# Convolution's tokens and attention's latents, 32 bytes further on in SBUF

## The chip, the cores and the metric

The kernel runs on one core of a Trainium2 chip. The metric is the device time of one execution, in microseconds (us). The engines are TensorE (PE; its weight loads, PEld, overlap its matmuls), VectorE (DVE), ScalarE (ACT), GpSimd (POOL) and SyncE (SP), which issues most of the DMAs. A matmul holds one operand still in the array (the stationary one, loaded by a weight load ahead of it) and streams the other (the moving one) past it. Both are read from SBUF.

## The reference

Two layers act on 256 tokens of width 2048, all in float32. The first layer mixes tokens with a Conformer convolution module, the second with multi-head latent attention; each is followed by an MLP with a squared ReLU.

```
x = x + conv_module(rms_norm(x))     # layer 0
x = x + sq_relu_mlp(rms_norm(x))
x = x + mla(rms_norm(x))             # layer 1
x = x + sq_relu_mlp(rms_norm(x))
return rms_norm(x)

conv_module:  u = h @ w_pw1 + b; u = a * sigmoid(gate)      # 2048 -> 2 x 2048
              u = causal depthwise conv, width 31
              u = silu(layer_norm(u)) @ w_pw2 + b
mla:          down = h @ w_in                               # c_q 512, c_kv 512, k_pe 64
              q  = rms_norm(c_q)  @ w_q_up                  # 16 heads x (128 + 64)
              kv = rms_norm(c_kv) @ w_kv_up                 # 16 heads x (128 + 128)
              softmax of (q_nope k_nope + q_pe k_pe), block-causal mask; @ v; @ w_o
sq_relu_mlp:  square(relu(h @ w1)) @ w2                     # 2048 -> 8192 -> 2048
```

## The kernel before

**Split products.** Every large product is made of float32r parts. A weight tile comes in by DMA (`raw`), ScalarE copies it to a rounded high part `hi`, and VectorE or GpSimd writes the remainder `lo = raw - hi`. The tokens have a high and a low part likewise. A product is then three matmuls: high by high, high by low, low by high. The pool `wpool` holds six `hi` and six `lo` buffers of 4096 bytes per partition.

**Turned tokens.** `open_xt` opens a pool on the right side of SBUF with four tiles `xt` of 8192 bytes per partition; `xh(k)` and `xl(k)` are the high and low parts of the k-th 128 channels for all 256 tokens. `to_T` fills them: TensorE turns 128x128 blocks against `ident`, ScalarE writes the high part (L201), VectorE the low one (L208). The pool is opened once at the start, and serves the convolution's first product, the first MLP and attention's first product. It is closed when attention opens its own right-hand pool `gp`, and opened again for the last MLP.

**Convolution.** The loop runs over 16 chunks c of 128 channels. For a chunk, `conv_mm` (L850 to L852) does 96 matmuls of 256 columns: 16 slices of the width, two halves (value and gate), three products; the weights stand still and `xh(k)` or `xl(k)` moves. `glu` makes the gated row `ub` from the two sums (ScalarE L872 and L880, GpSimd L881; for the last chunk VectorE L875). VectorE then does most of the 31 taps of the depthwise convolution (L952), after ScalarE has started the sum with tap 0 (L908) and some taps have gone to ScalarE and GpSimd (L885, L928, joined at L935). GpSimd writes nearly all low parts of the weights here (L170). Up to some 20 taps of earlier chunks may be left over (`REST`), and `to_tokens(c - 3)` (L990) lets TensorE turn a finished chunk between the matmuls of chunk c. The last chunk's taps are partly done by TensorE (L900). After the layer norm comes the second product, with 512 moving columns of weights (L195 to L197), whose results are added to the residual stream and prepared for the MLP as `xt` again.

**MLP.** Upwards, `xh` with `xl` (512 columns, L510) and `xh` alone (256 columns, L508) move past the weights. Downwards weights move (512 columns).

**Attention.** The first product has `xt` stationary and moves weights, in two halves of 288 columns for keys and values and 512 for queries. The normed latents are turned into `kvh`, `kvl` (keys and values) and `qh`, `ql` (queries), 128 x 4 x 256 each. From these come the keys of each head (L1412 to L1414: weights stationary, `kvh` and `kvl` moving), the queries (L1435 to L1437, `qh` and `ql` moving), and, through `mm3` (L195 to L197), values and rotary queries (the latents stationary, 256 columns of weights moving). `kpA`, `kpB` and `qpB` hold the rotary key with the mask, and the rotary query. The pieces of the next group of four heads are placed by hand between the scores of the current one.

**Placement.** Several pads fix where tiles start: `PAD_CONST`, `PAD_SMALL` and `PAD_RIGHT` in the outer pools, `PAD_SH` and `PAD_STATS` in the convolution's, `PAD_O` ahead of attention's outputs `oh` and `ol`. With the sizes of all tiles added up, `hi`, `lo`, `xt`, `sh`, `kvh`, `kvl`, `qh`, `ql`, `oh` and the MLP's tiles begin at addresses whose remainder modulo 256 is 64. A right-hand pool ends where the tile `pad_right` begins, and its tiles lie in it in the order in which they are made, so a tile made behind them moves them to lower addresses. The order of instructions on each engine is that of the program text (`manual_schedule`).

Of the kernel before, what the change touches and what calls it, by code (L numbers as in the profile page):

```python
# [10 lines left out]
F32 = mybir.dt.float32  # L11
# [7 lines left out]
P = 128  # L19
# [17 lines left out]
PAD_CONST = 24  # L37
PAD_SMALL = 32
PAD_RIGHT = 40
PAD_SH = 16  # L40
PAD_STATS = 48
PAD_O = 64
WB = 6
LOOK = WB // 2 - 1
LAST_PE = 22
# [37 lines left out]
def trunk_kernel(  # L83
# [49 lines left out]
    edge = ctx.enter_context(tc.tile_pool(name="edge", bufs=1, side="right"))  # L133
    pad_right = edge.tile([P, PAD_RIGHT], F32, name="pad_right")
    nc.gpsimd.memset(pad_right, 0.0)
# [3 lines left out]
    def nm(s):  # L139
        uid[0] += 1  # L140
        return f"{s}_{uid[0]}"
# [104 lines left out]
    def to_T(src, k0, hi, lo, gain, pt=None):  # L246

        pt = pt if pt is not None else tr_tile()
        for j in range(2):
            for t in range(T):  # L250
                nc.tensor.transpose(  # L251
                    pt[:, j * S + t * P : j * S + (t + 1) * P],
                    src[:, t, (k0 + j) * P : (k0 + j + 1) * P],
                    ident,
                )
        ps = [pt[:, j * S : (j + 1) * S] for j in range(2)]
        for j in range(2):
            hi_part(ps[j], hi(k0 + j), gain[:, k0 + j : k0 + j + 1])
        for j in range(2):
            lo_part(ps[j], hi(k0 + j), lo(k0 + j), gain[:, k0 + j : k0 + j + 1])  # L260
# [44 lines left out]
    def right_pool(name, bufs):  # L305

        xt_cx[0].close()
        xt_cx[0] = ExitStack()
        return xt_cx[0].enter_context(tc.tile_pool(name=name, bufs=bufs, side="right", reuse_waits="tile"))

    ctx.callback(lambda: xt_cx[0].close())

    def open_xt(name):
        pool = right_pool(name, 1)
        xt[:] = [
            pool.tile([P, KC // NNB, 2 * S], F32R, name=nm("xt")) for _ in range(NNB)
        ]

    xhl = lambda k: xt[k // 4][:, k % 4, :]
    xh = lambda k: xhl(k)[:, :S]  # L320
    xl = lambda k: xhl(k)[:, S:]
    open_xt("xt0")
    spare = []

    xh_kt = lambda k, t: xh(k)[:, t * P : (t + 1) * P]
# [2 lines left out]
    def residual_stage(last, gain, r_scale=None):  # L328


        ssq = small.tile([P, T, NNB], F32, tag="ssq", name=nm("ssq")) if last else None

        def add(n, ps, t):
            sl = slice(n * NB, (n + 1) * NB)
            if r_scale is None:
                nc.vector.tensor_tensor(xs[:, t, sl], ps[t], xs[:, t, sl], op=ALU.add)
            else:
                nc.vector.scalar_tensor_tensor(
                    out=xs[:, t, sl], in0=ps[t], scalar=r_scale[:, t : t + 1], in1=xs[:, t, sl],
                    op0=ALU.mult, op1=ALU.add,  # L340
                )

        def prepare(n, only=None):
            sl = slice(n * NB, (n + 1) * NB)
            if last:
                if gain is not None:
                    for j in range(2):
                        to_T(xs, 4 * n + 2 * j, xh, xl, gain)
                for t in range(T) if only is None else [only]:
                    nc.scalar.activation(spare[-1](), xs[:, t, sl], AF.Square, accum_out=ssq[:, t, n : n + 1])  # L350

        return ssq, add, prepare
# [441 lines left out]
    with ExitStack() as cx:  # L794
# [15 lines left out]
        cn = cv.tile([P, T, D], F32, tag="tok", name="cn")  # L810
        cv.tile([P, PAD_SH], F32, name="pad_sh")
        sh = cv.tile([P, KC, S], F32R, name="sh")
# [204 lines left out]
        with tc.manual_schedule():  # L1017
# [143 lines left out]
            for m in range(NP):  # L1161
# [17 lines left out]
                sl = slice(i * NB, (i + 1) * NB)  # L1179
                nc.vector.tensor_tensor(xs[:, t, sl], xs[:, t, sl], b2[:, sl], op=ALU.add)  # L1180

        ssq, add, prepare = residual_stage(True, g_mlp[0])
        for b in range(2):
            for t in range(T):
# [62 lines left out]
    with ExitStack() as cx:  # L1247
        at = cx.enter_context(tc.tile_pool(name="at", bufs=1, reuse_waits="tile"))
# [60 lines left out]
        def u_load(n):  # L1309
            if n < len(units):  # L1310
                srcs, shape = units[n]
                raw = raws[n] = wpool.tile(shape, F32, tag="raw", name=nm("raw"), bufs=3)
                for i, src in enumerate(srcs):
                    dst = raw if len(srcs) == 1 else raw[:, i : i + 1, :]
                    if len(src.shape) == 4:
                        dst = dst.rearrange("p j (h n) -> p j h n", h=src.shape[2])
                    nc.sync.dma_start(dst, src)
# [18 lines left out]
        def prefetch(n=9):  # L1336
            while pending and n > 0:
# [3 lines left out]
                if h == 1:  # L1341
                    u_load(u + 3)

        kvh = at.tile([P, KR // P, S], F32R, name="kvh")
        kvl = at.tile([P, KR // P, S], F32R, name="kvl")
        qh = at.tile([P, QR // P, S], F32R, name="qh")
# [15 lines left out]
        for i in range(2):  # L1362
            for j in range(HG):
                nc.scalar.activation(qpB[i][DR:, j, :], mq[DR:, :], AF.Copy)
        pad_o = at.tile([P, PAD_O], F32, name="pad_o")
        nc.gpsimd.memset(pad_o, 0.0)
# [202 lines left out]
        with tc.manual_schedule():  # L1569
# [123 lines left out]
            prefetch()  # L1693

        open_xt("xt1")
        ssq, add, prepare = residual_stage(True, g_mlp[1])
        for b in range(2):
# [82 lines left out]
```

## Time and profile before

| | us |
|---|---|
| median of 3 runs | 1940.86 |
| lowest, highest | 1940.85, 1940.98 |
| profiled execution | 1940.68 |
| its span | 1938.9 |

| engine | busy us | share of the span |
|---|---|---|
| TensorE matmuls | 1915.4 | 99% |
| TensorE weight loads | 1682.5 | 87% |
| VectorE | 1651.8 | 85% |
| ScalarE | 1204.8 | 62% |
| GpSimd | 223.7 | 12% |

The mean granted clock of TensorE was 0.998. The convolution's first product and taps fill some 20 to 220 us of the span, its second product the time up to some 320 us, the first MLP the time up to some 990 us, attention that up to some 1260 us, and the second MLP the rest.

A row of a group gives line, engine, operation, the tiles (out<-in), the shapes and the count, then the time in which any of them ran, the mean length of one in ns, and the engine's idle time ahead of them with what ended it. Matmuls overlap in the pipeline, so the mean length of one is more than its share of the time; the distance between starts, read from the timeline (start, length, engine, line, tiles, count), is that share. A row of windows gives the stretch, its length and the busy time of each engine, with the number of instructions.

### The profile page before, as it was taken

To read this page: it belongs to the slowest core of one execution; us is meant where nothing else is said; L and a number is where in the kernel's file an instruction comes from. 1 tells how busy PE (TensorE), PEld (TensorE's weight loads), DVE (VectorE), ACT (ScalarE), POOL (GpSimd) and SP (SyncE) were. 2 spreads that over 40 slices of the span, in tenths; PEclk is the share of its full clock that TensorE was granted. 3 is DMA by queue.
4 is the path that set the end of the run, shared out by engine and by line. 5 is a ranking of instruction groups with operands and counts; after the bars stand their busy time and mean duration, and the time that the engine had idled before them with its cause. 6 is when DMAs were issued, how large, how long until landed. Compare 5 with 4: busy or idle time off the path is not lost.

```text
span 1938.9 us, 28476 instructions
## 1 busy us (share of the span) xinstructions
PE 1915.4 (99%) x10778; PEld 1682.5 (87%) x10778; DVE 1651.8 (85%) x2372; ACT 1204.8 (62%) x1709; POOL 223.7 (12%) x183
## 2 busy tenths in 40 slices
PE   7999999999999999999999999999999999999998
PEld 7999888888888888888899998888888888888886
DVE  5999875789999999999976666557999999999887
ACT  5556654766666666666566665556766666666654
POOL 5999400000000000000001410000000000000000
PEclk9999999999999999999999999999999999999999
DMA  8666456857666667666646445765667666766663
GB/s 236 184 175 177 146 184 169 222 171 210 198 204 204 203 198 212 200 198 212 199 143 182 121 152 174 200 186 171 201 191 210 210 196 195 214 200 195 211 223 109
DMA packets 407113, 367.62 MB, mean 190 GB/s; under 512 B 15416, under 2 KB 351936, under 8 KB 406720
## 3 DMA queue, kind: packets, MB, share of 16 engines
q1 hardware_dynamic: 405952, 363.63, 62.8%
q10 hardware_dynamic: 1024, 2.17, 0.3%
q8 instruction: 84, 1.38, 0.3%
q14 instruction: 53, 0.43, 0.1%
HBM read 363.68 MB, written 2.10 MB: 189 GB/s over the span
## 4 chain that ended last, share of the span: by engine, by line
PE 98%; DVE 1%; DMA 1%; ACT 0%; issue 0%; DVEq 0%; ACTq 0%
PE acc L510 24%; PE acc L196 15%; PE acc L195 15%; PE acc L197 15%; PE acc L508 13%; PE acc L851 3%; PE acc L850 3%; PE acc L852 3%; PE acc L251 1%; PE sum L900 1%; PE acc L1435 0%; PE acc L1437 0%; PE acc L1436 0%; PE acc L1412 0%; PE acc L1414 0%; PE acc L1413 0%
## 5 line engine op out<-in xcount | busy, mean ns | idle before, releaser
L421 DVE TENSOR_TENSOR lo<-raw,hi 128x1024 fp32r<-128x1024 f32 (+1 forms) x512 | 571.1, 1122 | 90.1 <-ACT hi L420 81.7
L420 ACT ACTIVATE hi<-raw 128x1024 fp32r<-128x1024 f32 (+1 forms) x512 | 479.7, 970 | 66.9 <-PE acc L196 66.6
L510 PE MATMUL acc<-xt,hi 128*128 128x512 f32 x2048 | 503.2, 391 | 0.0
L510 PEld LDWEIGHTS acc<-xt,hi 128*128 128x128 f32 x2048 | 376.1, 188 | 72.5
L195 PE MATMUL acc<-hi,sh 128*128 128x512 f32 x930 | 362.7, 390 | 0.0
L197 PE MATMUL acc<-lo,sh 128*128 128x512 f32 x930 | 362.0, 389 | 0.0
L196 PE MATMUL acc<-hi,sl 128*128 128x512 f32 x802 | 312.0, 389 | 0.0
L508 PEld LDWEIGHTS acc<-xt,lo 128*128 128x128 f32 x2048 | 262.6, 191 | 10.0
L508 PE MATMUL acc<-xt,lo 128*128 128x256 f32 x2048 | 265.7, 283 | 0.0
L169 ACT ACTIVATE hi<-raw 128x1024 fp32r<-128x1024 f32 (+2 forms) x184 | 179.8, 1005 | 46.8 <-PE acc L196 43.0
L197 PEld LDWEIGHTS acc<-lo,sh 128*128 128x128 f32 x930 | 174.6, 188 | 36.2
L195 PEld LDWEIGHTS acc<-hi,sh 128*128 128x128 f32 x930 | 174.6, 188 | 36.0
L170 DVE TENSOR_TENSOR lo<-raw,hi 128x1024 fp32r<-128x1024 f32 (+2 forms) x118 | 132.8, 1146 | 68.5 <-ACT hi L169 62.8
L420 ACT ACTIVATE hi<-V 128x1024 fp32r<-128x1024 f32 x94 | 99.5, 1059 | 129.6 <-DVE V L716 114.8
L196 PEld LDWEIGHTS acc<-hi,sl 128*128 128x128 f32 x802 | 150.5, 188 | 31.2
L952 DVE SCALAR_TENSOR_TENSOR sum<-ub,w_dw,sum 128x256 f32<-128x256 f32 x400 | 163.3, 482 | 8.7 <-ACT sum L908 7.1
L170 POOL TENSOR_TENSOR lo<-raw,hi 128x1024 fp32r<-128x1024 f32 x66 | 157.7, 2409 | 24.4 <-ACT hi L169 24.4
L420 ACT ACTIVATE hi<-T 128x1024 fp32r<-128x1024 f32 x94 | 99.2, 1056 | 89.6 <-DVE T L704 77.2
L515 ACT ACTIVATE U<-acc 128x512 f32<-128x512 f32 x128 | 76.0, 593 | 117.6 <-PE acc L510 117.0
L850 PE MATMUL acc<-xt,hi 128*128 128x256 f32 x512 | 146.3, 286 | 0.0
L851 PE MATMUL acc<-xt,hi 128*128 128x256 f32 x512 | 145.0, 283 | 0.3 <-DVE xt L208 0.3
L852 PE MATMUL acc<-xt,lo 128*128 128x256 f32 x512 | 144.9, 283 | 0.0
(269 smaller groups left out, 2805.5 us busy)
## 6 DMA issues: line engine op xcount, KB each, us to landing
raw<-in_mlp_w SPq DMA_DIRECT2D x256, 1024.0 KB, 6.1
raw<-in_conv_w_pw SPq DMA_DIRECT2D x64, 512.0 KB, 5.5
raw<-in_conv_w_pw SPq DMA_DIRECT2D x16, 1024.0 KB, 5.1
raw<-in_mla_w_o SPq DMA_DIRECT2D x16, 1024.0 KB, 5.3
raw<-in_mla_w_kv_up SPq DMA_DIRECT2D x8, 1024.0 KB, 5.4
raw<-in_mla_w_in SPq DMA_DIRECT2D x8, 576.0 KB, 3.8
raw<-in_mla_w_in SPq DMA_DIRECT2D x4, 1024.0 KB, 7.1
raw<-in_mla_w_q_up SPq DMA_DIRECT2D x16, 256.0 KB, 5.1
```

The lines of the kernel that those rows point to most:

```text
L169: nc.scalar.activation(hi, raw[:, js, :], AF.Copy)
L170: eng.tensor_tensor(lo, raw[:, js, :], hi.bitcast(F32), op=ALU.subtract)
L195: nc.tensor.matmul(ps, sh, mh, start=start, stop=False)
L196: nc.tensor.matmul(ps, sl, mh, start=False, stop=False)
L197: nc.tensor.matmul(ps, sh, ml, start=False, stop=stop)
L420: nc.scalar.activation(parts[0], src, AF.Copy)
L421: nc.vector.tensor_tensor(parts[1], src, parts[0].bitcast(F32), op=ALU.subtract)
L508: nc.tensor.matmul(ps[0][:, :S], wl[:, j, :], xh(k), start=False, stop=False)
L510: nc.tensor.matmul(ps[0], wh[:, j, :], xhl(k), start=k == 0, stop=k == KC - 1)
L850: nc.tensor.matmul(o, wh[:, bs], xh(k), start=k == 0, stop=False)
L851: nc.tensor.matmul(o, wh[:, bs], xl(k), start=False, stop=False)
L852: nc.tensor.matmul(o, wl[:, bs], xh(k), start=False, stop=k == KC - 1)
```

## The change

The constant `PAD_XT` (56 floats, 224 bytes) and `PAD_KV` (8 floats, 32 bytes) are new, and `PAD_O` goes from 64 to 56 floats.

For the convolution the right-hand pool is now opened under the name `xtc`, with a pad tile behind the four `xt` tiles, which puts them 224 bytes lower: at remainder 96 modulo 256, 32 more than that of `hi` and `lo`. Ahead of the second product's additions to the residual stream the pool is closed and a new one, `xt0`, opened without a pad, so the MLP's and attention's `xt` stand where they stood before.

In attention, a pad of 32 bytes stands ahead of `kvh`, so `kvh`, `kvl`, `qh`, `ql`, `kpA`, `kpB` and the two `qpB` move up by 32 bytes, to remainder 96; `pad_o` is 32 bytes shorter, so `oh`, `ol` and all that follows stay where they were. The weights stay at 64. No matmul, copy or DMA is added or removed.

```
+PAD_XT = 56
+PAD_KV = 8
-PAD_O = 64
+PAD_O = 56
...
-    def open_xt(name):
+    def open_xt(name, pad=0):
         pool = right_pool(name, 1)
         xt[:] = [
             pool.tile([P, KC // NNB, 2 * S], F32R, name=nm("xt")) for _ in range(NNB)
         ]
+        if pad:
+            pool.tile([P, pad], F32, name=nm("pad_xt"))
...
-    open_xt("xt0")
+    open_xt("xtc", PAD_XT)
...
+        open_xt("xt0")
         ssq, add, prepare = residual_stage(True, g_mlp[0])
         for b in range(2):
             for t in range(T):
...
+        at.tile([P, PAD_KV], F32, name="pad_kv")
         kvh = at.tile([P, KR // P, S], F32R, name="kvh")
         kvl = at.tile([P, KR // P, S], F32R, name="kvl")
         qh = at.tile([P, QR // P, S], F32R, name="qh")
```

More of the change, by code (lines that the diff above doesn't have):

```diff
@@ L39 @@
 PAD_RIGHT = 40
+PAD_XT = 56
+PAD_KV = 8
 PAD_SH = 16
 PAD_STATS = 48
-PAD_O = 64
+PAD_O = 56
 WB = 6
@@ L311, in trunk_kernel, with open_xt @@
     ctx.callback(lambda: xt_cx[0].close())
-    def open_xt(name):
+    def open_xt(name, pad=0):
         pool = right_pool(name, 1)
@@ L317, in open_xt @@
         ]
+        if pad:
+            pool.tile([P, pad], F32, name=nm("pad_xt"))
     xhl = lambda k: xt[k // 4][:, k % 4, :]
@@ L321, in trunk_kernel @@
     xl = lambda k: xhl(k)[:, S:]
-    open_xt("xt0")
+    open_xt("xtc", PAD_XT)
     spare = []
@@ L1180, in trunk_kernel @@
                 nc.vector.tensor_tensor(xs[:, t, sl], xs[:, t, sl], b2[:, sl], op=ALU.add)
+        open_xt("xt0")
         ssq, add, prepare = residual_stage(True, g_mlp[0])
@@ L1342, in prefetch @@
                     u_load(u + 3)
+        at.tile([P, PAD_KV], F32, name="pad_kv")
         kvh = at.tile([P, KR // P, S], F32R, name="kvh")
```

## The prediction

> **What bounds the kernel.** I read the page first: its busy shares and the chain of work that ended last.
>
> ```profile
> PE 1915.4 (99%) x10778; PEld 1682.5 (87%) x10778; DVE 1651.8 (85%) x2372; ACT 1204.8 (62%) x1709; POOL 223.7 (12%) x183
> PE 98%; DVE 1%; DMA 1%; ACT 0%; issue 0%; DVEq 0%; ACTq 0%
> PE acc L510 24%; PE acc L196 15%; PE acc L195 15%; PE acc L197 15%; PE acc L508 13%; PE acc L851 3%; PE acc L850 3%; PE acc L852 3%; PE acc L251 1%; PE sum L900 1%; PE acc L1435 0%; PE acc L1437 0%; PE acc L1436 0%; PE acc L1412 0%; PE acc L1414 0%; PE acc L1413 0%
> ```
>
> TensorE is busy for 99% of the span and carries 98% of the chain, so a change of some nanoseconds in its matmuls counts wherever nothing else is equally full. The change does no arithmetic; it moves operands by 32 bytes, so the question is which matmuls it touches and what each costs from start to start. The groups by shape give the counts:
>
> ```profile
> L850 PE MATMUL acc<-xt,hi 128*128 128x256 f32 x512 | 146.3, 286 | 0.0
> L851 PE MATMUL acc<-xt,hi 128*128 128x256 f32 x512 | 145.0, 283 | 0.3 <-DVE xt L208 0.3
> L852 PE MATMUL acc<-xt,lo 128*128 128x256 f32 x512 | 144.9, 283 | 0.0
> ...
> L1412 PE MATMUL acc<-kvh,hi 128*128 128x256 f32 x64 | 18.4, 288 | 0.0
> L1435 PE MATMUL acc<-qh,hi 128*128 128x256 f32 x64 | 18.3, 287 | 0.0
> L195 PE MATMUL acc<-hi,kvh 128*128 128x256 f32 x64 | 18.3, 287 | 0.0
> ...
> L195 PE MATMUL acc<-hi,qh 128*128 128x256 f32 x32 | 9.1, 283 | 0.0
> ```
>
> Three lines of 512 make 1536 in the convolution. In attention each group shown stands for three products (high by high, high by low, low by high): 3 x (64 + 64 + 64 + 32) = 672. All have 256 columns. (The score products with kpA and kpB, 64 in number, are left out of the sum.)
>
> The durations of single matmuls overlap, so the price of one is its pitch, read from the timeline of TensorE: first and last start of an unbroken stretch. In the convolution:
>
> ```profile
> 195.72 0.28 PE L852 MATMUL acc<-xt,lo 128*128 128x256 f32 x1
> ...
> 205.08 0.28 PE L852 MATMUL acc<-xt,lo 128*128 128x256 f32 x1
> ```
>
> That is 26 triples, 78 matmuls in 9.36 us: 120 ns each. In attention's query products, 21 in 2.52 us, again 120 ns:
>
> ```profile
> 1060.92 0.28 PE L1435 MATMUL acc<-qh,hi 128*128 128x256 f32 x1
> ...
> 1063.44 0.28 PE L1435 MATMUL acc<-qh,hi 128*128 128x256 f32 x1
> ```
>
> Three more stretches say what 120 ns is made of: 512 columns, attention's first product with 288 columns, and transposes that only keep the array warm.
>
> ```profile
> 300.52 0.39 PE L196 MATMUL acc<-hi,sl__120 128*128 128x512 f32 x1
> ...
> 302.11 0.39 PE L197 MATMUL acc<-lo,sh 128*128 128x512 f32 x1
> ```
> ```profile
> 1012.07 0.30 PE L195 MATMUL acc<-hi,xt 128*128 128x288 f32 x1
> ...
> 1012.47 0.29 PE L195 MATMUL acc<-hi,xt 128*128 128x288 f32 x1
> ...
> 1012.87 0.30 PE L195 MATMUL acc<-hi,xt 128*128 128x288 f32 x1
> ```
> ```profile
> 220.80 3.00 PE L234 MATMUL acc<-ident 128*128 128x128 f32 x26
> ```
> ```profile
> L234 PE MATMUL acc<-ident 128*128 128x128 f32 x48 | 5.7, 273 | 0.0
> ```
>
> 512 columns: 7 steps in 1.59 us, 227 ns. So 256 further columns cost 107 ns, and a matmul of 256 is 107 ns of columns and 13 ns on top; 288 columns take 0.40 us per triple, 133 ns, the same 13 on top. The 26 transposes: (3.00 - 0.27 for the last one's length, the group's mean of 273 ns) / 25 = 109 ns, the shortest spacing with a weight load each. The 13 ns are what a placement of operands could touch.
>
> **What the trace knows of placement.** In the layout before, weights (hi, lo), xt, kvh, kvl, qh and ql all start at remainder 64 modulo 256, worked out from the pools' sizes, and slices move them by multiples of 256. One exception: the second half of the 288-column product starts 288 x 4 = 1152 bytes on, so its moving operand lies 128 away from the stationary one. Triples of the two halves alternate above, and both take 0.40 us. So 128 costs what 0 costs. No row has 32.
>
> A hint that the two streams do hinder each other is in the weight loads:
>
> ```profile
> L510 PEld LDWEIGHTS acc<-xt,hi 128*128 128x128 f32 x2048 | 376.1, 188 | 72.5
> L508 PEld LDWEIGHTS acc<-xt,lo 128*128 128x128 f32 x2048 | 262.6, 191 | 10.0
> L850 PEld LDWEIGHTS acc<-xt,hi 128*128 128x128 f32 x512 | 97.8, 191 | 0.0
> ...
> L1436 PEld LDWEIGHTS acc<-ql,hi 128*128 128x128 f32 x64 | 12.3, 192 | 0.0
> ```
>
> Between matmuls of 512 columns a load takes 188 ns, between those of 256 it takes 191 to 192, some 4 ns more.
>
> **The parts and their prices.** First, the pitch. Bounds: at best the 11 ns between 120 and 109 go; the rows of 128 bytes say 0; on the loss side the nearest row is the stretch of the loads, 4 ns, once more. I take a gain of 4 ns, the stretch of the loads, because it is the one row that shows the streams apart and together.
>
> Attention is TensorE's throughout:
>
> ```profile
> 1040.00:1160.00 120.00, 119.50 (x957) 116.77 (x956) 81.52 (x181) 75.93 (x186) 37.76 (x56) 1.00 0.46 138
> ```
>
> VectorE is busy 81.5 of 120 us, so a gain arrives in full: 672 x 4 ns = 2.7 us.
>
> The convolution is another matter. VectorE's taps run beside it, and its windows and timeline read (columns: length, then PE, PEld, DVE, ACT, POOL):
>
> ```profile
> 36.00:72.00 36.00, 36.00 (x303) 36.00 (x302) 32.33 (x77) 18.99 (x30) 34.07 (x22) 1.00 0.63 170
> 72.00:200.00 128.00, 128.00 (x1071) 128.00 (x1071) 127.47 (x329) 71.29 (x119) 120.53 (x79) 1.00 0.65 177
> ```
> ```profile
> 46.80 6.75 DVE L952 SCALAR_TENSOR_TENSOR sum<-ub,w_dw,sum 128x256 f32<-128x256 f32 x17 [1.10 <-ACT sum L908]
> ...
> 70.06 0.49 DVE L952 SCALAR_TENSOR_TENSOR sum<-ub,w_dw,sum 128x256 f32<-128x256 f32 x1 [1.45 <-ACT sum L908]
> ...
> 209.10 0.48 DVE L875 SCALAR_TENSOR_TENSOR ub<-acc,vecs,sg 128x256 f32<-128x256 f32 x1 [1.01 <-ACT sg L872]
> ```
>
> From 72 to 200 us VectorE has 0.5 us idle in 128: it is as full as TensorE. It waits for TensorE's chunks only at 46.8, 70.1 and 209.1 us. So TensorE's 1536 x 4 ns = 6.1 us don't arrive. VectorE can start earlier by what TensorE gains up to the chunk behind the wait at 70 us, the fourth: 4 x 96 x 4 ns = 1.5 us (less than the 2.55 us of idle in the two waits), and saves the 1.0 us at the end, where TensorE will be ahead. Together 2.5 us; late next are the taps, and TensorE then waits at to_tokens for VectorE's last tap of a chunk.
>
> Second, the separate pool. The convolution reads its tokens last at 208.2 us and the new pool's first write, which must wait for that, is at 279.75 us:
>
> ```profile
> L852 PE MATMUL acc<-xt,lo x512: 279/283/338, 19.8 to 208.2; 128*128 128x256 f32 x171
> ```
> ```profile
> 279.75 3.01 ACT L201 ACTIVATE xt<-acc,vecs 128x256 fp32r<-128x256 f32 x8
> ```
>
> 71 us cover it: nothing. No instruction or DMA is added (the pads are never written).
>
> Third, pad_kv takes 32 bytes and pad_o gives 32 back, so oh and ol stay put. kpB now ends 32 bytes inside a tile of squares that the MLP frees, so it waits for its last reader. qpB, right behind it on ScalarE, waits for that tile already, without idle time before it:
>
> ```profile
> 998.33 0.41 ACT L1361 ACTIVATE kpB<-scratch 64x256 fp32r<-64x256 f32 x1
> 998.65 1.62 ACT L1364 ACTIVATE qpB<-scratch 64x256 fp32r<-64x256 f32 x5
> ```
>
> Nothing again. Behind that in the queue stand the weight splits; they lose nothing.
>
> Sum: 2.7 + 2.5 = 5.2 us. The profiled execution took 1940.68 us (span 1938.9), 0.18 below the median of the runs: 1940.68 - 5.2 = 1935.5, against the median 1935.6 us.
>
> **The rivals.** (a) Placement doesn't matter to TensorE, as between 0 and 128. For: the triples of 0.40 us. Against: 13 ns on top of the columns and loads stretched by 4 ns, which something must cause. The time stays at 1940.9. [...]
>
> (b) Slower: 32 bytes make the streams meet more often than 0 does. In kvh's and qh's stationary use (288 of the 672) the moving weights lie 32 behind instead of ahead, so at least one of the two signs is likely worse than the other. For: everything in the layout stands at one remainder, so no row clears 32. With 4 ns lost, nothing cushions it: (1536 + 672) x 4 ns = 8.8 us, 1949.7 us. It decides from +1.8 ns: 2208 x 1.8 = 4 us, 0.2%.
>
> (c) The whole surplus goes, 120 to 109: attention 672 x 11 = 7.4; in the convolution the two waits (2.55), a first tap earlier by 96 x 11 ns (1.1) and the 1.0 at the end, 4.6 us: 1928.9. Against: then 13 ns would be collision alone, and 128 bytes remove none of them. [...]
>
> **How the numbers follow.** 0.2%, 3.9 us, is about what a measurement of this kernel can tell from no change. In the gain case the sum is 1.0 + (384 + 672) x d; it passes 3.9 at d = 2.7 ns. Gains from there to 11 ns, (c) included: 0.45, of which (c) 0.08. Rival (a) and shifts of under 2 ns: 0.30. Rival (b): 0.25. The range runs from (c), 1928.5, to a loss of 3 ns, 1947.5; beyond it lie the larger losses of (b), about 0.12, and little below. The likeliest case's own range is 1929 to 1937.
>
> **What the profile after would show.** Right: starts of L850 to L852 nearer than 120 ns (116), PEld of L850 and L1436 at 188, VectorE's waits at 46.8 and 70 us shorter, and TensorE waiting before L990 for VectorE in the convolution, while L1435's stretch keeps its gain whole. (a) would show 120 ns everywhere; (b) triples of over 0.37 us from both L850 and L1412, with VectorE's idle time growing. The prediction is wrong if the pitch doesn't move, or if it moves and VectorE turns out to follow (then the convolution gives up to 6 us instead of 2.5). Unmoved in any case: L510, L508 and the 512-column products.

## The result and the profile after

The changed kernel takes 1936.8 us (median of 14 runs, 1936.38 to 1938.62) against 1940.86 us (1940.75 to 1940.98 in the runs beside it): 0.9981 of the time before (95% interval 0.9973 to 0.9989), 4.1 us less. The forecast was 1935.6 us. Ten of the 14 runs lie at 1936.4 to 1936.9 us and four at 1938.1 to 1938.6; the profiled execution, 1938.23 us (span 1936.4), is one of the four; its trace shows the granted clock at 0.50 for 3.4 us, to which the experiments below put the difference down.

With the added lines the convolution's L850 to L852 are now L854 to L856, the taps L956, TensorE's taps L904, the MLP L514 and L512, the keys L1418 to L1420 and the queries L1441 to L1443.

The page's engine line, and its chain by engine and by line:

```profile
PE 1910.2 (99%) x10778; PEld 1676.8 (87%) x10778; DVE 1651.4 (85%) x2372; ACT 1206.3 (62%) x1709; POOL 223.8 (12%) x183
PE 89%; DVE 8%; ACT 1%; DMA 1%; issue 0%; POOL 0%; DVEq 0%; ACTq 0%
PE acc L514 24%; PE acc L198 15%; PE acc L197 15%; PE acc L199 15%; PE acc L512 13%; DVE sum L956 6%; PE acc L855 1%; PE acc L854 1%; PE acc L856 1%; PE acc L253 1%; PE sum L904 1%; PE acc L1554 0%; DMA xs<-in_x 0%; ACT hi L171 0%; PE acc L1418 0%; PE acc L1420 0%
```

The same 10778 matmuls, but TensorE is busy 5.2 us less, and 8% of the chain now belongs to VectorE: its taps (L956) have taken the chain over from the convolution's products. The weight loads, by shape:

```profile
L514 PEld LDWEIGHTS acc<-xt,hi 128*128 128x128 f32 x2048 | 376.1, 188 | 72.5
L512 PEld LDWEIGHTS acc<-xt,lo 128*128 128x128 f32 x2048 | 262.6, 191 | 10.0
...
L855 PEld LDWEIGHTS acc<-xt,hi 128*128 128x128 f32 x512 | 96.3, 188 | 1.2 <-DVE xt L210 1.2
L854 PEld LDWEIGHTS acc<-xt,hi 128*128 128x128 f32 x512 | 96.2, 188 | 0.0
```

The convolution's loads fell from 191 to 188 ns, the MLP's (L514, L512), whose operands were not moved, stayed at 188 and 191. TensorE's timeline (start, length, engine, line, tiles, count) gives the pitches, and the end of the convolution:

```profile
191.18 0.28 PE L855 MATMUL acc<-xt,hi 128*128 128x256 f32 x1
...
195.74 0.28 PE L855 MATMUL acc<-xt,hi 128*128 128x256 f32 x1
...
204.03 0.28 PE L856 MATMUL acc<-xt,lo 128*128 128x256 f32 x1
206.37 6.70 PE L904 MATMUL sum<-ub,dg 128*128 128x256 f32 x22 [2.06 <-DVE ub L879]
...
1055.52 0.28 PE L197 MATMUL acc<-hi,qh 128*128 128x256 f32 x1
...
1058.36 0.28 PE L1441 MATMUL acc<-qh,hi 128*128 128x256 f32 x1
...
1061.86 0.28 PE L1441 MATMUL acc<-qh,hi 128*128 128x256 f32 x1
```

In the convolution 39 matmuls take 4.56 us, 117 ns each instead of 120. In attention the queries, where the latents move, take 3.50 / 30 = 117 ns; with the latents stationary it is 2.84 / 24 = 118 ns. The windows (length, then busy time and count of PE, PEld, DVE, ACT, POOL, the granted clock, DMA share, GB/s) show who is full:

```profile
36.00:72.00 36.00, 36.00 (x311) 36.00 (x310) 33.29 (x79) 19.99 (x30) 35.04 (x23) 1.00 0.63 173
72.00:200.00 128.00, 128.00 (x1100) 128.00 (x1099) 128.00 (x332) 74.47 (x128) 121.74 (x79) 1.00 0.66 183
...
204.00:206.00 2.00, 0.31 (x3) 0.11 (x1) 2.00 (x7) 1.42 (x2) 1.04 (x3) 1.00 0.87 356
206.00:208.00 2.00, 1.63 (x5) 1.34 (x6) 2.00 (x7) 1.65 (x5) 2.00 (x1) 0.71 0.04 8
208.00:210.00 2.00, 2.00 (x7) 1.55 (x6) 2.00 (x6) 1.96 (x3) 1.92 (x4) 0.50 0.00 0
210.00:212.00 2.00, 2.00 (x10) 1.78 (x9) 2.00 (x6) 0.00 (x0) 2.00 (x2) 0.94 0.00 0
```

From 72 to 200 us TensorE does 1100 matmuls instead of 1071, and VectorE's row shows no idle time any more. Then TensorE has nothing to do for 2.06 us (ahead of L904), and behind that gap its granted clock is 0.71, 0.50 and 0.94 in three windows of 2 us: the missing 0.29, 0.50 and 0.06 of 2 us each are 1.7 us of work lost, as much as 3.4 us at half speed. VectorE's timeline, with its idle time before each group in brackets:

```profile
46.35 6.76 DVE L956 SCALAR_TENSOR_TENSOR sum<-ub,w_dw,sum 128x256 f32<-128x256 f32 x17 [0.78 <-ACT sum L912]
...
68.98 0.49 DVE L956 SCALAR_TENSOR_TENSOR sum<-ub,w_dw,sum 128x256 f32<-128x256 f32 x1 [0.81 <-ACT sum L912]
...
185.63 0.49 DVE L939 TENSOR_TENSOR sum<-sum,tp 128x256 f32<-128x256 f32 x1
...
205.79 0.52 DVE L879 SCALAR_TENSOR_TENSOR ub<-acc,vecs,sg 128x256 f32<-128x256 f32 x1
```

The third row stood before the change at:

```profile
187.79 0.42 DVE L935 TENSOR_TENSOR sum<-sum,tp 128x256 f32<-128x256 f32 x1
```

Against the rows before, VectorE is ahead by 0.45 us, by 1.08, by 2.16, and at the last chunk's `ub` by 3.31; there its wait of 1.01 us is gone.

Counted from each trace's first matmul, the last matmul of the convolution's first product starts at 191.85 us instead of 196.17 (4.3 earlier), the second product at 213.45 instead of 215.19 (1.7 earlier, the drop of the clock included). Attention, from its first product with the latents to its last value product, takes 157.74 instead of 158.59 us.

### The profile page after: what moved, and what is told of

Same layout as the page of the kernel before. It is cut to its first block, busy times and chain, and to the rows that moved or that the text cites. A ratio compares the mean times of both kernels' runs of the same rounds, so it can differ in the third digit from the quotient of the medians.

```text
span 1936.4 us, 28476 instructions
## 1 busy us (share of the span) xinstructions
PE 1910.2 (99%) x10778; PEld 1676.8 (87%) x10778; DVE 1651.4 (85%) x2372; ACT 1206.3 (62%) x1709; POOL 223.8 (12%) x183
## 4 chain that ended last, share of the span: by engine, by line
PE 89%; DVE 8%; ACT 1%; DMA 1%; issue 0%; POOL 0%; DVEq 0%; ACTq 0%
PE acc L514 24%; PE acc L198 15%; PE acc L197 15%; PE acc L199 15%; PE acc L512 13%; DVE sum L956 6%; PE acc L855 1%; PE acc L854 1%; PE acc L856 1%; PE acc L253 1%; PE sum L904 1%; PE acc L1554 0%; DMA xs<-in_x 0%; ACT hi L171 0%; PE acc L1418 0%; PE acc L1420 0%
## 5 line engine op out<-in xcount | busy, mean ns | idle before, releaser
L514 PE MATMUL acc<-xt,hi 128*128 128x512 f32 x2048 | 503.2, 391 | 0.0
L514 PEld LDWEIGHTS acc<-xt,hi 128*128 128x128 f32 x2048 | 376.1, 188 | 72.5
L512 PEld LDWEIGHTS acc<-xt,lo 128*128 128x128 f32 x2048 | 262.6, 191 | 10.0
L512 PE MATMUL acc<-xt,lo 128*128 128x256 f32 x2048 | 265.7, 283 | 0.0
L956 DVE SCALAR_TENSOR_TENSOR sum<-ub,w_dw,sum 128x256 f32<-128x256 f32 x400 | 164.2, 517 | 7.1 <-ACT sum L912 6.0
L854 PE MATMUL acc<-xt,hi 128*128 128x256 f32 x512 | 144.4, 282 | 0.0
L855 PE MATMUL acc<-xt,hi 128*128 128x256 f32 x512 | 143.0, 279 | 1.0 <-DVE xt L210 1.0
L856 PE MATMUL acc<-xt,lo 128*128 128x256 f32 x512 | 143.0, 279 | 0.3 <-POOL lo L172 0.3
```

Source lines behind the costliest of these rows:

```text
L512: nc.tensor.matmul(ps[0][:, :S], wl[:, j, :], xh(k), start=False, stop=False)
L514: nc.tensor.matmul(ps[0], wh[:, j, :], xhl(k), start=k == 0, stop=k == KC - 1)
L854: nc.tensor.matmul(o, wh[:, bs], xh(k), start=k == 0, stop=False)
L855: nc.tensor.matmul(o, wh[:, bs], xl(k), start=False, stop=False)
L956: nc.vector.scalar_tensor_tensor(out=out, in0=ubs[c][:, w : w + S], scalar=tap(c, w), in1=pcs[c], op0=ALU.mult, op1=ALU.add)
```

## The experiments

**One part alone.** Three kernels take the change apart. e1_conv_only leaves attention as it was:

```
-        at.tile([P, PAD_KV], F32, name="pad_kv")
-PAD_O = 56
+PAD_O = 64
```

> Only the convolution's tokens are moved; attention is as before. Theory (the step of 32 bytes shortens the pitch from 120 to some 116.5 ns, and VectorE's taps take most of the convolution's share): faster by 1.7 to 3 us, 1938 to 1939, with L854 to L856 at 116 to 117 ns and L1435's pitch at 120. Rival (the convolution's gain arrives in full): 5 us, 1935.5. Rival (the gain is attention's alone): 1940.9.

e2_attention_only is the kernel before with the pads in attention alone:

```
+        at.tile([P, PAD_KV], F32, name="pad_kv")
-PAD_O = 64
+PAD_O = 56
```

> Only attention's latents are moved, the convolution's pool is as before. Theory: the 672 matmuls gain 1.4 us by the profile after, a wait for the softmax weights gives 0.6 back: faster by 0.8 to 1.5 us, 1939.4 to 1940.1. My prediction's step (672 x 4 ns in full): 2.7 us, 1938.2. Rival (latents don't matter): 1940.9.

e3_pool_alone has the separate pool for the convolution, but with a pad of 256 bytes, which leaves the remainder unchanged:

```
-PAD_XT = 56
+PAD_XT = 64
-        at.tile([P, PAD_KV], F32, name="pad_kv")
-PAD_O = 56
+PAD_O = 64
```

> The separate pool with a pad of 256 bytes instead of 224, so that the tokens stay at the weights' remainder; attention as before. Theory (placement does it): 1940.9, pitch 120 ns. Rival (the pool's own tiles, freed earlier or later, do it): faster by 1 us or more at a pitch of 120 ns.

| kernel | median us (lowest, highest) | ratio to before |
|---|---|---|
| e1_conv_only | 1938.89 (1937.24, 1939.37) | 0.9987 [0.9979, 0.9996] |
| e2_attention_only | 1939.96 (1939.83, 1940.15) | 0.9996 [0.9987, 1.0004] |
| e3_pool_alone | 1940.77 (1940.59, 1940.91) | 1.0000 [0.9991, 1.0009] |

The kernel before took 1940.76 us beside them. The pool swap costs nothing (e3). Attention's part gives 0.8 us; its interval alone does not tell that from no change, but attention lasts 157.74 us in its trace, as in the changed kernel, and none of its eleven runs reaches the 1940.58 us of the fastest run before. The convolution's part stands at two levels: five of eleven runs at 1937.2 to 1937.7, 3.1 to 3.6 us faster, and six at 1938.9 to 1939.4. The profiled execution of e1 is one of the five, and its windows, with the columns as above, show the same gap with no drop of the clock behind it:

```profile
204.00:206.00 2.00, 0.21 (x2) 0.00 (x1) 2.00 (x7) 1.42 (x2) 1.00 (x3) 1.00 0.85 346
206.00:208.00 2.00, 1.74 (x8) 1.55 (x9) 2.00 (x6) 1.76 (x5) 2.00 (x1) 1.00 0.03 8
208.00:210.00 2.00, 2.00 (x11) 1.76 (x10) 2.00 (x6) 1.84 (x2) 1.92 (x4) 1.00 0.00 0
```

Its 22 matmuls behind the gap take 5.02 us instead of 6.70. The 1.7 us between them is the distance of the two levels.

**The gap filled.** e4_keep_warm is the changed kernel with 18 transposes into an unused tile where TensorE is idle:

```
                 conv_load(n + 3)
+                if c == KC:
+                    keep_warm(ident, N_WARM_UB)      # 18
                 glu(c - 1)
```

> The changed kernel, with 18 transposes of the identity (some 2 us) put on TensorE behind the last chunk's products, where the profile after shows TensorE idle for 2.06 us and the granted clock at one half for 3.4 us afterwards. Theory (that drop costs the longer runs some 1.7 us, and only some runs have it): all runs at the level of the shorter ones or below, 1936.0 to 1936.8, none near 1938. Rival (the two levels come from elsewhere): runs near 1938.2 stay.

It takes 1936.53 us (1936.34 to 1936.81, eleven runs), ratio 0.9978 [0.9969, 0.9987]; none is near 1938. TensorE's timeline and the windows:

```profile
203.95 2.13 PE L237 MATMUL acc<-ident 128*128 128x128 f32 x18
206.19 5.02 PE L905 MATMUL sum<-ub,dg 128*128 128x256 f32 x22
```
```profile
206.00:208.00 2.00, 1.89 (x9) 1.62 (x9) 2.00 (x6) 1.83 (x5) 2.00 (x1) 1.00 0.00 0
208.00:210.00 2.00, 2.00 (x11) 1.74 (x10) 2.00 (x7) 1.77 (x2) 1.92 (x4) 1.00 0.00 0
```

The clock stays at 1.00 and the upper level is gone; the second product starts at 211.75 us from the first matmul. So without the drop the convolution's part is worth 215.19 - 211.75 = 3.4 us. Only one execution per kernel has its clock over time on record. Of the other runs there is the mean clock to three digits, of which 3.4 us at half speed are 0.0009: in e1 the five shorter runs have 0.998 (four) and 0.999, the six longer ones 0.997 (five) and 0.998; of the changed kernel's runs all four longer ones have 0.998, and six of the ten shorter ones 0.999. With the equal distance and e4 that speaks for a drop in every run at the upper level.

**VectorE relieved.** e6_taps_before and e7_taps_after are the kernels before and after with VectorE's last four taps of 15 chunks left out:

```
-            left[c] = list(range(w + n, W))
+            left[c] = list(range(w + n, W - (4 if c < KC - 1 else 0)))
```

> The kernel before, but VectorE leaves out four of the taps in each of the first 15 chunks of the convolution (60 taps of 0.4 us). Theory (TensorE and VectorE are about equally full before): TensorE alone sets the pace, faster than before by 1 to 4 us at the end of the convolution. It is the base for the next kernel.

> The changed kernel with the same four taps left out in 15 chunks. Theory (VectorE's taps hold back the convolution's gain): without them the 1536 matmuls gain 3.4 ns each in full, 5.2 us, and attention 0.8: 6 us below the kernel before with the same taps left out. Rival (the rest was lost elsewhere, to the clock or to the pool's swap): the difference stays at 4 us.

| kernel | median us (lowest, highest) | ratio to before |
|---|---|---|
| e6_taps_before | 1940.80 (1940.68, 1940.91) | 1.0000 [0.9990, 1.0009] |
| e7_taps_after | 1935.83 (1935.51, 1936.26) | 0.9974 [0.9964, 0.9985] |

The same window of e6 and then of e7, with VectorE's busy time as the third number behind the length:

```profile
72.00:200.00 128.00, 128.00 (x1072) 128.00 (x1071) 111.21 (x286) 71.28 (x119) 120.40 (x79) 1.00 0.65 177
```
```profile
72.00:200.00 128.00, 128.00 (x1100) 128.00 (x1099) 114.30 (x293) 74.42 (x128) 121.75 (x79) 1.00 0.66 182
```

Some 16 us of free VectorE time gain nothing in the kernel before. The expected gain there was missed: VectorE was nearly full and still set nothing. After the change the relief is worth 0.9 us in the convolution (second product at 210.87 us from the first matmul, against 211.75 in e4). Over the whole kernel e7 is 5.0 us faster than e6. That is neither the 6 us of the theory, which took 3.4 ns for each of the 1536 matmuls where the products' end comes 4.3 us earlier (2.8 ns each), nor the 4 us of the rival. The waits of TensorE for `ub` (us in total, times, longest) say the same, first in the kernel before, then in e7:

```profile
PE sum L900 <- DVE ub L875: 1.1, 1, 1.1
```
```profile
PE sum L904 <- DVE ub L879: 1.1, 1, 1.1
```

In both the wait is 1.1 us, the time that the last chunk's gate takes anyhow; in the changed kernel it is 2.1 us. The 1.0 between is what VectorE is late.

**Other distances.** e5_sweep gives each group of four slices of the convolution's tokens another distance from the weights (modulo 256: 64, 128, 192, 224), and leaves attention as it was before the change:

```
+PAD_XTS = (0, 16, 16, 8)
...
+            if pad and PAD_XTS[i]:
+                pool.tile([P, PAD_XTS[i]], F32, name=nm("pad_xt"))
```

> In the convolution each of the four token tiles has its own distance from the weights modulo 256: 64, 128, 192 and 224 bytes for slices 0-3, 4-7, 8-11 and 12-15. Read is the pitch in each quarter of a chunk's matmuls. Theory (a collision only where both streams start at the same place of a 128-byte period, as 0 and 128 cost the same): 128 at 120 ns, the other three at 115 to 118 ns. Rival (32 bytes ahead is special): 64, 128, 192, 224 all at 119 ns or more.

One execution took 1938.3 us. TensorE's timeline, where a tile of four slices lasts 24 matmuls, first at distance 64, then at 128:

```profile
124.59 0.28 PE L857 MATMUL acc<-xt,hi 128*128 128x256 f32 x1
...
127.42 0.28 PE L857 MATMUL acc<-xt,hi 128*128 128x256 f32 x1
...
130.26 0.28 PE L857 MATMUL acc<-xt,hi 128*128 128x256 f32 x1
```

2.83 us and 2.84 us, 118 ns each. Over all starts the means are 117.8 at 64, 118.5 at 128, 117.6 at 192 and 118.3 at 224 (117 at 32, 120 at 0). Neither the theory (120 at 128) nor the rival (119 or more everywhere) held: in this stream of 256-column matmuls 0 alone is bad.

e8_xt_all puts `xt` at 32 in the MLPs too:

```
-PAD_RIGHT = 40
-PAD_XT = 56
+PAD_RIGHT = 96
+PAD_XT = 0
...
-        open_xt("xt0")
```

> The tokens stand 32 bytes from the weights everywhere, in the two MLPs and attention's first product too. Theory (each matmul of 256 or 512 columns gains about 3 ns, as the stretch of a weight load is the same): the MLPs' 2048 + 2048 matmuls gain 8 to 14 us, 1923 to 1929. Rival (only a weight load that is back to back with the last one is stretched, so 512 columns gain nothing): 256-column ones gain 3 ns each, some 6 us, 1931. Rival (512 columns lose what 256 gain): 1937 or above.

1944.79 us (1944.24 to 1946.33), ratio 1.0023 [1.0013, 1.0032]: slower than before the change by 4 us. TensorE's timeline, before the change and then in e8:

```profile
396.88 3.82 PE L510 MATMUL acc<-xt,hi 128*128 128x512 f32 x16
400.53 2.08 PE L508 MATMUL acc<-xt,lo 128*128 128x256 f32 x16
```
```profile
399.91 3.90 PE L514 MATMUL acc<-xt,hi 128*128 128x512 f32 x16
403.64 1.56 PE L512 MATMUL acc<-xt,lo 128*128 128x256 f32 x12
```

From the first start to the second 16 matmuls of 512 columns take 3.73 us instead of 3.65, 233 ns instead of 228. The 256-column ones of the MLP gain some 2 ns, and the 512-column ones lose more: each MLP takes 3.8 us longer. (The larger `PAD_RIGHT` moves attention's pool `gp` too; attention takes 157.66 us, as in the changed kernel.)

e10_mlp_sweep, with e4's transposes, spreads the distances over the MLPs (the last argument is the pad ahead of each of the four tiles, in floats):

```
+        open_xt("xt0", 8, (0, 16, 16, 8))     # 64, 128, 192, 224
...
+        open_xt("xt1", 24, (0, 8, 16, 16))    # 0, 32, 96, 160
```

> The changed kernel with the 18 transposes, and in the MLPs and attention's first product each token tile at a distance of its own: first MLP 64, 128, 192 and 224 bytes for slices 0-3, 4-7, 8-11, 12-15; second MLP 0, 32, 96 and 160. Read is the pitch by tile. Theory (512 columns lose at any distance that is no multiple of 128, as they lost at 32): L517's like at 230 ns or more for 32, 64, 96, 160, 192, 224 and at 227 for 0 and 128; 256 columns at 117 to 119 for all but 0. Rival (32 alone is bad for 512 columns): 227 at some of the other distances, which would then gain in the MLPs.

One execution took 1944.61 us. Its timeline, four matmuls at distances 64 and four at 128, then four at 0 and four at 32:

```profile
411.90 2.02 PE L517 MATMUL acc<-xt,hi 128*128 128x512 f32 x8
...
1408.24 2.01 PE L517 MATMUL acc<-xt,hi 128*128 128x512 f32 x8
1410.09 1.13 PE L515 MATMUL acc<-xt,lo 128*128 128x256 f32 x8
```

The latter take 1.85 us for 8, 231 ns on average. Split over all starts (means, ns):

| distance | 0 | 32 | 64 | 96 | 128 | 160 | 192 | 224 |
|---|---|---|---|---|---|---|---|---|
| 512 columns | 227.6 | 234.1 | 233.0 | 233.8 | 230.6 | 233.5 | 234.6 | 232.9 |

No distance is better than 0 for 512 columns. That 128 costs anything was not expected. The columns of the table were read on different slices, though, 64 and 0 on slices 0 to 3, 128 and 32 on 4 to 7, 192 and 96 on 8 to 11, 224 and 160 on 12 to 15. In the kernel before, where the distance is 0 throughout, these four groups take 226.7, 226.7, 232.5 and 227.7 ns; the third comes right behind the 256-column matmuls. Against the same slices 64, 32, 160 and 224 cost 5 to 7.5 ns and 128 costs 4, but 192 and 96 only 1 to 2; e8, at 32, takes 232 ns on slices 8 to 11 too.

Nor does the distance alone set the pitch. The second MLP's 256-column matmuls take 119.6, 119.8 and 119.2 ns in e10 at 32, 96 and 160, where e8 has 117.5 at 32 for the same matmuls: where the run of matmuls begins with slices at 0, the gain is mostly gone on the later slices too. In the first MLP, at 64 to 224, they take some 118. Why is open.

**Work moved from VectorE to TensorE.** e11_rebalance and e12_more_on_pe try to win the 0.9 us back by more of the last chunk's taps on TensorE. Beside e4's transposes (4 in e11, 18 in e12):

```
-LAST_PE = 22
+LAST_PE = 24
-LAST_REST = (20, 17, 0)      # e11 alone
+LAST_REST = (20, 22, 0)
```

> The kernel with the transposes (4 of them instead of 18), where VectorE leaves 22 taps instead of 17 ahead of the last chunk's gated row, so that TensorE's own taps start some 2 us earlier, and TensorE does 24 taps of the last chunk instead of 22. Theory (VectorE holds back the end of the convolution by 0.9 us): 0.5 to 0.9 us below the kernel with 18 transposes (4.2 us faster than before), 1935.6 to 1936.1. Rival (TensorE's own taps set that end): the same or slower than with 18 transposes, 1936.5 to 1937.5.

> The kernel with 18 transposes, and only TensorE's share of the last chunk's taps goes from 22 to 24. Theory (VectorE's taps end the convolution): up to 0.8 us faster than with 22, 1935.7 to 1936.3. Rival (TensorE's own taps, started late, set that end): 0.8 us slower, 1937.3.

They take 1937.18 us (1937.13 to 1937.7; 0.9982 [0.9973, 0.9991]) and 1937.68 us (1937.47 to 1938.14; 0.9984 [0.9975, 0.9993]), 0.65 and 1.15 us more than e4. VectorE's timeline in e11, and in e12:

```profile
205.28 0.49 DVE L880 SCALAR_TENSOR_TENSOR ub<-acc,vecs,sg 128x256 f32<-128x256 f32 x1 [0.97 <-ACT sg L877]
```
```profile
210.55 0.43 DVE L940 TENSOR_TENSOR acc<-acc,tp 128x256 f32<-128x256 f32 x1 [0.63 <-POOL tp L933]
...
212.16 0.43 DVE L1005 BATCH_NORM_STATS2 stats<-tr 128x6 f32<-128x256 f32 x1 [0.79 <-PE tr L995]
```

In e11 VectorE is early and waits 0.97 us for the gate; in e12 it waits for GpSimd's product, and for turned blocks that stand behind TensorE's added taps. The expected gain of e11 did not come.

**The wait in attention.** e13_weights_earlier is e4 with the scaling of a head's softmax weights one piece earlier in the program:

```
                     piece(todo.pop(0))
+                    weights(h)
                     prefetch(1)
                     piece(todo.pop(0))
...
-                    weights(h)
                     prefetch(1)
```

> The kernel with 18 transposes, and in attention VectorE scales a head's softmax weights ahead of the next weight split instead of behind it, so that the scaling falls into VectorE's wait for ScalarE. Theory (a wait of 0.9 us for the softmax weights took part of attention's gain): that wait goes from TensorE's list, and the time is 0.6 to 1.1 us below the 1936.5 of the kernel with 18 transposes. Rival (the wait moves to another releaser, ScalarE's exponentials or the split that is now later): 1936.3 to 1937.

What it is aimed at shows in TensorE's waits between 1040 and 1160 us, of the kernel before and of the changed one, and in VectorE's timeline after the change:

```profile
PE acc L1539 <- DVE pr L1533: 0.4, 1, 0.4
```
```profile
PE acc L1545 <- DVE pr L1539: 1.1, 2, 1.0
```
```profile
1085.03 0.81 DVE L172 TENSOR_TENSOR lo<-raw,hi 128x512 fp32r<-128x512 f32 x1 [1.49 <-ACT hi L171]
1085.77 0.41 DVE L1429 COPY vv<-acc 128x256 f32<-128x256 f32 x1
1086.10 0.15 DVE L1536 RECIPROCAL zs<-zs 128x2 f32<-128x2 f32 x1
1086.29 0.55 DVE L1539 TENSOR_SCALAR pr<-pr,zs 128x128 f32<-128x128 f32 x2
```

The scaling (L1539) stands in VectorE's queue behind a weight remainder that waits 1.49 us for ScalarE. TensorE's wait for it was 0.4 us before the change and is 1.1 us after it; e2 has 1.1 us as well. e13 takes 1934.85 us (1934.57 to 1935.03; six runs), ratio 0.9969 [0.9957, 0.9981], 1.7 us less than e4, where 0.6 to 1.1 were expected. Its list of TensorE's waits in that stretch is empty, and so is its idle time:

```profile
1040.00:1160.00 120.00, 120.00 (x972) 117.52 (x970) 84.47 (x185) 79.19 (x189) 38.73 (x56) 1.00 0.47 139
```

Attention takes 155.92 us instead of 157.73 (e4): 1.4 us of that are the two gaps ahead of the softmax weights' transposes, and 0.4 the transposes themselves, which now follow each other more closely. It is the best kernel of the study, 6.0 us faster than before. The same move on the kernel before was not tried, so how much of the 1.7 us is gain of the change set free, and how much an older loss, stays open.

## Why the prediction was right or wrong

**The mechanism held.** The pitch of the moved matmuls fell by some 3 ns where tokens or latents move and by 1.6 ns where the latents are stationary (forecast 4 for all), and the loads beside the convolution's went from 191 to 188 ns. With the pool swapped but the distance kept, nothing moved (e3), so it is the placement. The prediction had no row at 32 bytes, and took the size from that stretch alone. Rival (a), no effect, would have left 1940.9 us; rival (b), a loss, fell in both signs: 117 ns with the latents moving, 118 with the weights moving 32 behind. Rival (c), the whole 11 ns, fell at 117 instead of 109. Placement does matter to TensorE here: 120 or 117 ns at 256 columns, 227 to 235 at 512. The argument from the 128-byte rows was sound for its shape of 288 columns, but doesn't carry over: e5 has 118.5 ns at 128.

**The pool and the pads at nothing: right.** e3 measures the swap at 0.0 us. The write of `kpB` has no idle time before it in the changed kernel either.

**Attention, 2.7 us: mis-sized.** e2 and the marks show 0.8 to 0.9. Two steps failed. The larger is the price, 4 ns for all 672: the matmuls gained 1.5 us (384 with the latents moving at 2.8 ns, 288 with them stationary at 1.6, over all starts), 1.2 less. The other is "so a gain arrives in full": one gap ahead of the transposes of the softmax weights, which grew from 0.68 to 1.25 us from start to start, took 0.6 back. VectorE's mean of 81.5 in 120 us hid that a single short operation on it stands on the path; the row to read was TensorE's list of waits in that window.

**The convolution, 2.5 us: too small.** Measured are 3.4 us without the drop of the clock. The forecast had 1.5 up to the wait at 70 us and 1.0 at the end; counted from the first matmul it became 1.2 there, 1.2 at the last `ub`, and 1.0 in between. "It waits for TensorE's chunks only at 46.8, 70.1 and 209.1 us" was misread: the trace before has five more waits for ScalarE's start of a sum, of 0.10 us each, ending at 93.5, 117.0, 140.5, 163.9 and 187.4 us. They are the 0.5 us of idle time in the window. Each gave 0.2 us when it went (VectorE's lead in the raw rows grows from 1.08 to 2.16 us over the five), twice what it showed. VectorE's records overlap (1085.77 + 0.41 is behind 1086.10), so its busy time covers idle time of tenths of a us. "As full as TensorE" was read as "sets the time as well": e6 shows that it did not. TensorE's own gain was 4.3 us, and VectorE holds back only 0.9 of it.

**Late next: wrong place.** There is no wait at `to_tokens` in the chunks (TensorE is busy 128.00 of 128 us). VectorE's lateness collects, and falls due once, at L904, as 1.0 us.

**Not in the sum: the clock.** In the profiled run the gap ahead of L904 is followed by half speed for 3.4 us, which costs 1.7; the three other long runs of the 14 are put down to the same, by e4 and their mean clock. Without it the steps add up to 3.4 + 0.8 = 4.2, and the ten runs of the lower level lie 4.0 to 4.5 us below the kernel before. The forecast's 5.2 was too high in attention by 1.9 and too low in the convolution by 0.9. These errors have opposite signs and partly cancel, so that the total lies within some 1 us of the forecast is in part luck: the direction, the matmuls concerned and the limit set by VectorE were reasoned, the two sizes were not right.

## What to carry to other kernels

The distance between the two operands of a matmul in SBUF, modulo 256 bytes, is worth up to 7 ns per float32r matmul here, with opposite signs by shape: move the 256-column pairs off 0, leave the 512-column pairs on it, and measure each shape apart before moving a tile that serves both. Where two engines are both full, ask which one's waits on the other grow; time freed in one may arrive nowhere, as in e6, and a gain in TensorE may stop at one operation queued behind a stalled one on an engine that has a third of its time free. After each gain look for the gap where it collected: fill or reorder that gap before judging the change.

## What was not expected of the hardware

- At 512 columns equal remainders are the best place (228 ns over a run of 16) and 32 bytes cost some 5 ns; at 256 columns, in the convolution, they are the worst (120), and every other distance tried gives 117 to 118.5. Which part of the chip makes the sign turn is open.
- Behind a gap of 2.06 us in TensorE the granted clock fell to 0.50 for 3.4 us in the profiled run of the changed kernel, and not behind nearly the same gap in another (e1's, 2.05 us, kept 1.00). Why one of the two runs dropped and the other did not is not shown.
- 18 transposes of an idle tile, 2.1 us of work for nothing, kept the clock at 1.00 in e4 at no cost: the second product starts at 211.75 us from the first matmul, in e1's run without a drop at 211.81.
